# Recurrence gates of a hybrid layer as pairs of 64-row matmuls, with an explicit order of steps

## The chip, the cores and the metric

The kernel runs on one core of one Trainium2 chip. The metric is device microseconds of one execution, as a median over runs. Engines are named as in the profile: PE (TensorE matmuls), PEld (its weight loads), DVE (VectorE), ACT (ScalarE), POOL (GpSimd), SP (SyncE, which issues most DMAs). A trailing q ("SPq") is an engine's sequencer, which issues DMAs and waits.

## The reference

One layer on 512 positions of width 1024, in float32. A normalised input goes through one large projection whose columns serve three mixers (pooling, a gated linear recurrence, stick-breaking attention) and three sets of gates; the mixers' outputs are projected, gated, summed, projected and added to the input; a SwiGLU feed-forward follows. The change lies in the recurrence:

```python
def rglru_mixer(u, conv_w, conv_b, w_rg, b_rg, w_ig, b_ig, lru_lambda):
    ...
    xc = conv_b + conv_w[0] * up[:, 0:S]
    for k in range(1, CONV_WIDTH):              # 4 taps, causal, per channel
        xc = xc + conv_w[k] * up[:, k:k + S]
    xb = xc.reshape(B, S, LRU_BLOCKS, LRU_BLOCK)    # 16 blocks of 64 channels
    r = jax.nn.sigmoid(jnp.einsum('bshi,hij->bshj', xb, w_rg)... + b_rg)
    i = jax.nn.sigmoid(jnp.einsum('bshi,hij->bshj', xb, w_ig)... + b_ig)
    log_a = (-LRU_C * r) * jax.nn.softplus(-lru_lambda)
    a = jnp.exp(log_a)
    mult = jnp.sqrt(-jnp.expm1(2.0 * log_a))
    b = mult * (i * xc)
    _, h = lax.associative_scan(combine, (a, b), axis=1)   # h[t] = a[t] h[t-1] + b[t]
```

## The kernel before

Channels lie on the 128 partitions, positions along the free dimension. Every large product is made of three matmuls (`mm3`): both operands are split into a rounded part (fp32r, "h" or "hi") and a residue ("l" or "lo"), and h·h, h·l and l·h are summed in PSUM. Splitting a weight costs an ACT instruction (`whi`, L99) and a DVE instruction (`wlo`, L100). Weights come in half-chunks of 512 KB through SP's DMA queue; a list `specs` gives their order, and `weights` keeps about three of them made ahead, at a scheduling priority 200 instructions earlier (`AHEAD`).

The program is written for a scheduler: every engine's order follows from the order in which instructions are emitted, shifted by `tc.high_priority(n)` to n instructions earlier, and by what is ready and which buffers are free in the scheduler's own reckoning. [...]

The recurrence has four chunks of 256 channels, two halves j of 128 channels each. `lru_chunk(c)` emits the projection matmuls (four steps of 12 matmuls, one step per weight half and j) into one PSUM tile (`ps_lru`), then small steps follow as closures in the list `bg`; after each step of 12 matmuls `tick` takes one closure from the list, or two where it holds more than 8. The steps are: the first tap with bias (L529), three more taps (`conv`, L536), the split (`xch` L542, `xcl` L543), for each j the two gates (`gates`: three matmuls for r, three for i, into the tile `lg`; sigmoids L553), `tanh` (L557, L560), then in `lru_late` exponent and square root (L569, L572), `lru_decay` (L577, L578), `lru_input` (L582, L583), the scan (L589) and a store to DRAM on POOL's queue (L593). A gate weight holds two blocks of 64 x 64 on the diagonal of a 128 x 128 matrix whose other half is zero.

Between the four chunks stand the chunks of the second branch's gates (`gate1`), then the seven-product query, key and value projections (`tok_product`, products named 11, 12, S2, S1, S3, S4, 22), which need sums of weights on DVE (L148) and of the normalised input (`prepare_t`). PSUM holds four tiles of two banks (`pb`); SBUF tiles of 4 KB per partition come from tags w (8), t (8) and b (13).

At the start, `warm` matmuls run while the first loads come. The first product (L610) goes over eight slices k of the input: `xt` slice k, its scaled and rounded form `hu` (L362, L363), and weights `whi`, `wlo` (L380, L383, later L99, L100). The vector constants `vt` are loaded in two parts, the first weights for k = 0 in two parts.

Of the kernel before, what the change touches and what calls it, by code (L numbers as in the profile page):

```python
# [8 lines left out]
F32 = mybir.dt.float32  # L9
# [17 lines left out]
NEG = -1.0e30  # L27
WARM = 7
# [5 lines left out]
PAD = 104  # L34
# [28 lines left out]
def layer_kernel(ctx: ExitStack, tc: tile.TileContext, x, xt, vecs, w_in, w_pool, w_rg, w_ig,  # L63
# [113 lines left out]
    for n in (0, 1, 4, 2, 3, 5, 6, 7):  # L177
        if n < 4:
            add_lru(n)
        else:  # L180
            add_gate(1, n - 4)
# [151 lines left out]
    with ExitStack() as first:  # L333
# [34 lines left out]

# [3 lines left out]
        src0 = cols(w_in, 0, 2, 5120, 512)  # L372
        for k in range(2):
            load_xt(k)
            for n in ((0, 2),) if k else ((0, 1), (1, 2)):
                q = slice(256 * n[0], 256 * n[1])
                if n == (0, 1):
                    nc.scalar.dma_start(vt[:, 0:8], vecs[:, 0:8])
                (nc.scalar if n == (0, 1) else nc.sync).dma_start(raw0[:, k, q], src0[:, k, q])
                dve.tensor_copy(hi0[:, k, q], raw0[:, k, q])  # L380
            if k == 0:
                nc.sync.dma_start(vt[:, 8:], vecs[:, 8:])
            dve.tensor_tensor(lo0[:, k, :], raw0[:, k, :], hi0[:, k, :].bitcast(F32), ALU.subtract)  # L383
            make_h(k)
# [125 lines left out]
        lw = {}  # L510

        def load_lru_weights():
            for nm, src in (("r", w_rg), ("i", w_ig)):
                raw = wp.tile([P, 8, P], F32, tag="raw", name="rawl" + nm)
                nc.gpsimd.memset(raw, 0.0)
                bd = src.rearrange("(t two) i j -> two i t j", two=2)
                for two in range(2):
                    q = slice(64 * two, 64 * two + 64)
                    nc.sync.dma_start(raw[q, :, q], bd[two])
                hi, lo = w4([8, P], f"lwh{nm}", F32R), w4([8, P], f"lwl{nm}", F32R)  # L520
                act(hi, raw, AF.Copy)
                dve.tensor_tensor(lo, raw, hi.bitcast(F32), ALU.subtract)
                lw[nm] = (hi, lo)

        def lru_chunk(c):
            pair = chan_chunk(("lru", c), hn, 1, pb, True)
            u, xc = pair, b4([2, S], f"xc{c}")
            for j in range(2):
                act(xc[:, j, :], pair[:, j, :], AF.Identity, scale=vcol("conv_w", 24 + 2 * c + j),  # L529
                    bias=vcol("conv_b", 2 * c + j))  # L530
# [9 lines left out]
            def split():  # L540
                st["h"], st["l"] = b4([2, S], f"xch{c}", "b", F32R), b4([2, S], f"xcl{c}", "b", F32R)
                act(st["h"], xc, AF.Copy)  # L542
                dve.tensor_tensor(st["l"], xc, st["h"].bitcast(F32), ALU.subtract)  # L543
                st["r"], st["i"] = b4([2, S], f"lr{c}"), b4([2, S], f"li{c}")

            def gates(j):
                ps = pb.tile([P, 2, S], F32, tag="mm", name=f"lg{c}{j}")
                for n, (nm, bn) in enumerate((("r", "b_rg"), ("i", "b_ig"))):
                    hi, lo = lw[nm]
                    ct = 2 * c + j  # L550
                    mm3(ps[:, n, :], hi[:, ct, :], lo[:, ct, :], st["h"][:, j, :], st["l"][:, j, :],
                        True, True)
                    act(st[nm][:, j, :], ps[:, n, :], AF.Sigmoid, bias=vcol(bn, ct))  # L553
# [8 lines left out]
            return [conv, split] + [nothing] * (2 + c // 2) + [lambda: gates(0), lambda: gates(1), tanh]  # L562
# [12 lines left out]
        def lru_decay(c):  # L575
            e, t = lru[c]["r"], lru[c]["t"]
            dve.scalar_tensor_tensor(t, e, 1.0, t, ALU.add, ALU.mult)  # L577
            act(t, t, AF.Identity, scale=-1.0, bias=1.0)  # L578
# [18 lines left out]
        def lru_late(cs):  # L597
            out = [lambda: lru_exp(cs)]
            for f in (lru_decay, lru_input, lru_scan, lru_store):
                out += [lambda f=f, c=c: f(c) for c in cs]  # L600
            return out
# [27 lines left out]
        bg.extend(lru_chunk(0))  # L629
        bg.extend(lru_chunk(1))  # L630
        bg.extend(lru_late((0, 1)))
        gate1(0)
        bg.extend(lru_chunk(2))
        bg.extend(lru_chunk(3))
        bg.extend(lru_late((2, 3)))
        gate1(1)
        gate1(2)
        bg.extend(prepare_t())
# [50 lines left out]
        for t in range(3):  # L689
# [15 lines left out]
            for nm in ORDER:  # L705
# [17 lines left out]
                else:  # L723
                    final((1, 0), ps["22"])
# [611 lines left out]
```

## Time and profile before

| | |
|---|---|
| median of 3 runs | 939.86 us (939.56 to 939.95) |
| the profiled execution | 940.17 us, span 938.4 us |
| granted TensorE clock | 1.00 |
| HBM read, written | 107.01 MB, 16.25 MB |

The times in a trace count from the span's start. In the rows of stages, an engine's figure is its busy time in that stretch, with the number of instructions behind it; in the groups, the figures are total busy time, mean ns of one, and the engine's idle time just before them with what ended it. In the list of waits the three figures are total us, times, longest.

### The profile page before, as it was taken

The numbers are of one execution on the slowest core, as the hardware profiler recorded it, in microseconds if no ns is written. First come the engines' busy times: TensorE is split into PE (matmuls) and PEld (weight loads), VectorE is DVE, ScalarE is ACT, GpSimd is POOL, SyncE is SP. The second block draws the span as 40 slices with busy tenths as digits, with TensorE's granted clock in tenths as the row PEclk, the third lists the DMA queues.
The fourth block names the chain that finished last, engine by engine and source line by source line (L and its number), as shares of the span: only waits on it lengthen the run. The fifth ranks groups of instructions, "written<-read, shape, count | busy, mean of one in ns | idle before, by whom it ended". The sixth has DMA issues, their size and how long they took to land.

```text
span 938.4 us, 13033 instructions
## 1 busy us (share of the span) xinstructions
PE 927.4 (99%) x5089; PEld 798.2 (85%) x5089; DVE 702.6 (75%) x877; ACT 491.6 (52%) x660; POOL 43.1 (5%) x71
## 2 busy tenths in 40 slices
PE   8999999999999999999999999999999999999998
PEld 6887878888878888788888878889999999988898
DVE  6895859877696699866865545699888888787465
ACT  6557689445665465645633324454554555653232
POOL 1100000122211000000000000000000000000000
PEclk9999999999999999999999999999999999999999
DMA  9483434552714943256422334345533334523001
GB/s 327 127 286 92 133 113 158 193 190 71 244 63 139 283 120 124 65 161 182 143 91 89 104 123 155 91 131 147 148 92 93 110 111 128 168 93 109 1 28 64
DMA packets 127022, 124.12 MB, mean 132 GB/s; under 512 B 7408, under 2 KB 105968, under 8 KB 126960
## 3 DMA queue, kind: packets, MB, share of 16 engines
q1 hardware_dynamic: 122784, 108.99, 38.0%
q0 software_dynamic: 3888, 14.16, 4.6%
q8 instruction: 40, 0.66, 0.3%
q14 instruction: 22, 0.18, 0.1%
q10 hardware_dynamic: 288, 0.14, 0.0%
HBM read 107.01 MB, written 16.25 MB: 131 GB/s over the span
## 4 chain that ended last, share of the span: by engine, by line
PE 93%; DVE 4%; issue 1%; ACT 1%; DMA 0%; POOL 0%; SPq 0%; DVEq 0%; POOLq 0%; ACTq 0%
PE ps_y L1148 11%; PE ps_x L1148 8%; PE ps_q L683 7%; PE ps_br L225 4%; PE ps_br L227 4%; PE ps_br L226 4%; PE ps_gate L226 3%; PE ps_gate L227 3%; PE ps_gate L225 3%; PE ps_d L225 3%; PE ps_d L227 3%; PE ps_d L226 3%; PE ps_dy L1148 2%; PE ps_gate L610 2%; PE ps_dx L1148 2%; PE ps_pool L225 2%
## 5 line engine op out<-in xcount | busy, mean ns | idle before, releaser
L99 ACT ACTIVATE whi<-raw 128x1024 fp32r<-128x1024 f32 x93 | 98.4, 1058 | 151.4 <-PE ps_br L226 46.2
L100 DVE TENSOR_TENSOR wlo<-raw,whi 128x1024 fp32r<-128x1024 f32 x93 | 113.6, 1222 | 70.1 <-ACT whi L99 65.2
L1138 ACT ACTIVATE wh_S<-w_S 128x1024 fp32r<-128x1024 f32 x44 | 46.6, 1061 | 56.6 <-PE ps_y L1148 25.4
L1139 DVE TENSOR_TENSOR wl_S<-w_S,wh_S 128x1024 fp32r<-128x1024 f32 x44 | 53.6, 1221 | 12.8 <-ACT wh_S L1138 12.6
L1138 ACT ACTIVATE wh<-w 128x1024 fp32r<-128x1024 f32 x33 | 35.1, 1062 | 49.0 <-issue 12.9
L100 DVE TENSOR_TENSOR wlo<-qw,whi 128x1024 fp32r<-128x1024 f32 x36 | 43.9, 1221 | 20.6 <-ACT whi L99 20.5
L1139 DVE TENSOR_TENSOR wl<-w,wh 128x1024 fp32r<-128x1024 f32 x33 | 40.3, 1222 | 17.4 <-ACT wh L1138 17.4
L99 ACT ACTIVATE whi<-qw 128x1024 fp32r<-128x1024 f32 x36 | 38.0, 1056 | 25.9 <-PE ps_q L683 13.7
L225 PE MATMUL ps_gate<-HH,whi 128*128 128x512 f32 x128 | 50.0, 391 | 0.0
L227 PE MATMUL ps_gate<-HH,wlo 128*128 128x512 f32 x128 | 49.9, 389 | 0.0
L226 PE MATMUL ps_gate<-HL,whi 128*128 128x512 f32 x128 | 49.8, 389 | 0.0
L225 PE MATMUL ps_d<-ah,whi 128*128 128x512 f32 x112 | 43.6, 391 | 0.0
L226 PE MATMUL ps_d<-al,whi 128*128 128x512 f32 x112 | 43.6, 389 | 0.0
L227 PE MATMUL ps_d<-ah,wlo 128*128 128x512 f32 x112 | 43.6, 389 | 0.0
L1126 DVE TENSOR_TENSOR w_S<-w,w 128x1024 f32<-128x1024 f32 x22 | 26.9, 1223 | 3.3 <-PE ps_d L226 2.9
L227 PEld LDWEIGHTS ps_gate<-HH,wlo 128*128 128x128 f32 x128 | 24.0, 188 | 5.1
L225 PEld LDWEIGHTS ps_gate<-HH,whi 128*128 128x128 f32 x128 | 24.0, 188 | 5.0
L226 PEld LDWEIGHTS ps_gate<-HL,whi 128*128 128x128 f32 x128 | 24.0, 188 | 4.9
L1126 DVE TENSOR_TENSOR w_S<-w,w_S 128x1024 f32<-128x1024 f32 x22 | 26.9, 1223 | 0.6
L901 DVE TENSOR_TENSOR_SCAN E<-K,zero 128x511 f32<-128x511 f32 (+3 forms) x32 | 25.5, 813 | 1.1 <-ACT K L896 1.1
L225 PE MATMUL ps_out<-mth,whi 128*128 128x512 f32 x64 | 25.0, 390 | 0.9 <-DVE g L310 0.9
L225 PE MATMUL ps_br<-yph,whi 128*128 128x512 f32 x64 | 25.6, 400 | 0.0
(642 smaller groups left out, 3016.5 us busy)
## 6 DMA issues: line engine op xcount, KB each, us to landing
raw<-in_w_in_dram SPq DMA_DIRECT2D x39, 512.0 KB, 4.6
qw<-in_w_in_dram SPq DMA_DIRECT2D x24, 512.0 KB, 4.7
raw<-in_w_branch_dram SPq DMA_DIRECT2D x24, 512.0 KB, 3.5
w<-in_w_ffn_gate_dram SPq DMA_DIRECT2D x36, 256.0 KB, 3.7
w<-in_w_ffn_up_dram SPq DMA_DIRECT2D x36, 256.0 KB, 4.5
raw<-in_w_ffn_down_dram SPq DMA_DIRECT2D x14, 512.0 KB, 3.5
qd<-r POOLq DMA_DIRECT2D x12, 512.0 KB, 3.6
at<-qd SPq DMA_DIRECT2D x24, 256.0 KB, 5.3
```

The lines of the kernel that those rows point to most:

```text
L99: act(hi, raw, AF.Copy)
L100: dve.tensor_tensor(lo, raw, hi.bitcast(F32), ALU.subtract)
L225: nc.tensor.matmul(ps, lh, rh, start=start, stop=False, skip_group_check=skip)
L226: nc.tensor.matmul(ps, lh, rl, start=False, stop=False, skip_group_check=skip)
L227: nc.tensor.matmul(ps, ll, rh, start=False, stop=stop, skip_group_check=skip)
L610: nc.tensor.matmul(pss[n // 2][n % 2], w[:, k % 2, n * P:(n + 1) * P], hu[k][x_], start=k == 0 and w is wh and x_ == 0, stop=k == KT - 1 a ...
L683: nc.tensor.matmul(ps[:, a, :], b_[:, k, ts_], a_[:, kk, :], start=first and n == k == 0, stop=n == 2 and k == 3, skip_group_check=True)
L901: dve.tensor_tensor_scan(E[:, f - 1:c0 + n - 1][:, ::-1], K[:, f:c0 + n][:, ::-1], zero[:, 0:1].to_broadcast([P, c0 + n - f]), 1.0, ALU.mu ...
L1126: dve.tensor_tensor(t, raw[c, x], raw[c, y], op)
L1138: act(h, raw[c, nm], AF.Copy)
L1139: dve.tensor_tensor(l, raw[c, nm], h.bitcast(F32), ALU.subtract)
L1148: nc.tensor.matmul(o, a[:, w, k, :], b[:, k, :], start=first and n == k == 0, stop=n == 2 and k == 3, skip_group_check=True)
```

## The change

- Gates: the weights of r and i of one block share a 64-row, 128-column tile. For the block on partitions 0 to 63 its columns are r then i, for the block on 64 to 127 i then r, so that r comes out on the block's own partitions and i on the others. Each of the three products is then a pair of 64-row matmuls into the two banks of a tile. A half has two 64-partition sigmoids for r and two for i; the i sigmoid moves its result to the other partitions, and its bias is loaded swapped into `bigx`. The gate weights take two tiles instead of four, and need no zeros.
- First tap, rounding of xc, and the decay's last step for the first two chunks are on DVE instead of ACT; taps and split run at priority `EARLY`.
- The order of steps is written out around the chunks; input and scan of the last chunks move behind product S3 of the first projection. The third chunk of the recurrence comes ahead of `gate1(0)`.
- Head: `vt` is loaded whole and first on SP's queue; the first weights are loaded whole, for k = 0 on ACT's queue.

```diff
-        for k in range(2):
-            load_xt(k)
-            for n in ((0, 2),) if k else ((0, 1), (1, 2)):
-                q = slice(256 * n[0], 256 * n[1])
-                if n == (0, 1):
-                    nc.scalar.dma_start(vt[:, 0:8], vecs[:, 0:8])
-                (nc.scalar if n == (0, 1) else nc.sync).dma_start(raw0[:, k, q], src0[:, k, q])
-                dve.tensor_copy(hi0[:, k, q], raw0[:, k, q])
-            if k == 0:
-                nc.sync.dma_start(vt[:, 8:], vecs[:, 8:])
+        nc.sync.dma_start(vt, vecs)
+        for k in range(2):
+            load_xt(k)
+            (nc.sync if k else nc.scalar).dma_start(raw0[:, k, :], src0[:, k, :])
+            dve.tensor_copy(hi0[:, k, :], raw0[:, k, :])
...
+            raw = wp.tile([P, 8, P], F32, tag="raw", name="rawl")
+            for n, src in enumerate((w_rg, w_ig)):
                 bd = src.rearrange("(t two) i j -> two i t j", two=2)
                 for two in range(2):
-                    q = slice(64 * two, 64 * two + 64)
-                    nc.sync.dma_start(raw[q, :, q], bd[two])
+                    q, o = LH[two], LH[(n + two) % 2]
+                    nc.sync.dma_start(raw[q, :, o], bd[two])
...
+            for two in range(2):
+                nc.sync.dma_start(bigx[LH[1 - two], :], big[LH[two], :])
...
-            for j in range(2):
-                act(xc[:, j, :], pair[:, j, :], AF.Identity, scale=vcol("conv_w", 24 + 2 * c + j),
-                    bias=vcol("conv_b", 2 * c + j))
+            with tc.high_priority(EARLY):
+                for j in range(2):
+                    dve.tensor_scalar(xc[:, j, :], pair[:, j, :], vcol("conv_w", 24 + 2 * c + j),
+                                      vcol("conv_b", 2 * c + j), ALU.mult, ALU.add)
...
-                act(st["h"], xc, AF.Copy)
+                dve.tensor_copy(st["h"], xc)
...
             def gates(j):
+                ct = 2 * c + j
                 ps = pb.tile([P, 2, S], F32, tag="mm", name=f"lg{c}{j}")
-                for n, (nm, bn) in enumerate((("r", "b_rg"), ("i", "b_ig"))):
-                    hi, lo = lw[nm]
-                    ct = 2 * c + j
-                    mm3(ps[:, n, :], hi[:, ct, :], lo[:, ct, :], st["h"][:, j, :], st["l"][:, j, :],
-                        True, True)
-                    act(st[nm][:, j, :], ps[:, n, :], AF.Sigmoid, bias=vcol(bn, ct))
+                for n, (w, x_) in enumerate((("h", "h"), ("h", "l"), ("l", "h"))):
+                    for two in range(2):
+                        q = LH[two]
+                        nc.tensor.matmul(ps[:, two, :], lw[w][q, ct, :], st[x_][q, j, :],
+                                         start=n == 0, stop=n == 2)
+                for two in range(2):
+                    q, o = LH[two], LH[1 - two]
+                    act(st["r"][q, j, :], ps[q, two, :], AF.Sigmoid, bias=vcol("b_rg", ct)[q, :])
+                    act(st["i"][q, j, :], ps[o, two, :], AF.Sigmoid, bias=bigx[o, ct:ct + 1])
...
+        c0, s0, g0, t0 = lru_chunk(0)
+        bg.extend([c0, s0, nothing, nothing])
+        c1, s1, g1, t1 = lru_chunk(1)
+        bg.extend([c1, s1, g0, t0])
+        c2, s2, g2, t2 = lru_chunk(2)
+        bg.extend([c2, s2, g1, t1])
         gate1(0)
+        bg.extend([lambda: lru_exp((0, 1)), g2] + late_of(lru_decay, 0, 1))
+        c3, s3, g3, t3 = lru_chunk(3)
+        bg.extend([c3, s3, t2] + late_of(lru_input, 0))
         gate1(1)
+        bg.extend(late_of(lru_input, 1) + [g3, t3, lambda: lru_exp((2, 3))])
         gate1(2)
+        for f, cs in ((lru_scan, (0, 1)), (lru_store, (0, 1)), (lru_decay, (2, 3)), (lru_input, (2,))):
+            bg.extend(late_of(f, *cs))
         bg.extend(prepare_t())
         gate1(3)
```

48 lines of the change are left out of this document (26 added, 22 removed).

## The prediction

> **What bounds the kernel now.** I read the page's first part, then the busy time by stage around the changed steps, then who waited for whom on PE and DVE, and last the order of single instructions at the places that these named.
>
> ```profile
> span 938.4 us, 13033 instructions
> PE 927.4 (99%) x5089; PEld 798.2 (85%) x5089; DVE 702.6 (75%) x877; ACT 491.6 (52%) x660; POOL 43.1 (5%) x71
> core 0: us, PE busy (x) PEld busy (x) DVE busy (x) ACT busy (x) POOL busy (x), PEclk, DMA share, GB/s
> 51.00:76.00 25.00, 25.00 (x112) 20.70 (x111) 24.40 (x30) 14.61 (x17) 1.45 (x2) 1.00 0.83 273
> 76.00:100.00 24.00, 24.00 (x105) 19.09 (x104) 10.33 (x11) 20.82 (x27) 0.72 (x1) 1.00 0.28 88
> 100.00:125.00 25.00, 23.49 (x103) 18.94 (x102) 24.09 (x26) 13.95 (x16) 1.45 (x2) 1.00 0.48 147
> 125.00:146.00 21.00, 21.00 (x92) 16.93 (x91) 10.45 (x10) 20.20 (x25) 0.73 (x1) 1.00 0.50 159
> 146.00:180.00 34.00, 34.00 (x151) 28.15 (x150) 31.00 (x28) 22.95 (x25) 5.16 (x6) 1.00 0.41 133
> sum 129.00, PE 127.49 PEld 103.82 DVE 100.27 ACT 92.54 POOL 9.52; mean PE 25.50 PEld 20.76 DVE 20.05 ACT 18.51 POOL 1.90
> ```
>
> The recurrence lies between 51 and 180 us. PE is the bound there, with one gap (23.49 of 25 us in 100 to 125), at the granted clock 1.00. VectorE is uneven: 24.4, 10.3, 24.1, 10.5, 31.0 us; where it is full, ScalarE has room, and the other way about. So an instruction taken off PE is worth its spacing, not its duration, and work moved to VectorE is free only as long as VectorE's idle 129 - 100.3 = 28.7 us can be used.
>
> ```profile
> 168.16 5.44 PE ps_q L683 x24
> 640.15 2.83 PE ps_y L1148 x24
> 75.00:146.00 71.00, 13.91 (x48) 8.49 (x48) 10.89 (x16) 1.00 0.41 129
> 118.77 0.39 PE L225 MATMUL ps_gate<-HH,whi 128*128 128x512 f32 x1
> 120.66 0.50 PE L225 MATMUL lg<-xch,lwhr 128*128 128x512 f32 x1 [1.51 <-ACT xch L542]
> 76.71 0.39 PE L225 MATMUL ps_gate<-HH,whi 128*128 128x512 f32 x1
> 76.97 0.50 PE L225 MATMUL lg<-xch,lwhi 128*128 128x512 f32 x1
> 77.31 0.39 PE L226 MATMUL lg<-xcl,lwhi 128*128 128x512 f32 x1
> PEld lg L225 <- ACT lr L553: 1.5, 5, 0.4
> ```
>
> First two: pieces of the chain, start, length, count. A 512-column matmul with its own weight load takes 5.44 / 24 = 0.227 us of PE, a 256-column one 2.83 / 24 = 0.118 us. The third is the stage table for the gate tile lg alone: 48 matmuls (and 48 loads). The next two show PE's gap: 1.51 us, because the rounding xch sat behind the convolution. The last four show a smaller loss: the weight load of the i gate waits for the sigmoid of the r gate, five times, and the next matmul then starts 0.34 us later instead of 0.227, since its load was not taken ahead.
>
> **The change, part by part.**
>
> *Gates.* 48 matmuls of 128 rows (half of each weight is zeros) become 48 of 64 rows, in 24 pairs; the two of a pair use different halves of the array's rows and different PSUM banks. No row of this trace shows a 64-row matmul. One end: no overlap, 48 x 0.227 = 10.9 us as now. Other end: a pair takes one spacing, 24 x 0.227 = 5.4 us. Each still has its own load of 128 columns; the 256-column row shows that a load fits into 0.118 us, so a pair needs 2 x 0.118 = 0.236 us for its loads, 24 x 0.236 = 5.7 us in all. I take that, nearest to a row: -5.2 us.
> [...]
>
> *Changing between full and half rows.* `both` puts 12 half-row matmuls in one place, four times, so there are 8 changes, more if the scheduler mixes them with other matmuls, as it did with lg and ps_gate at 120 us. Lower end 0. Upper end: the last matmul has to run out (0.39 - 0.227 = 0.16 us) and the next load isn't taken ahead (0.34 - 0.227 = 0.11 us), 8 x 0.27 = 2.2 us. I take the running out alone, 8 x 0.16 = +1.3 us.
> [...]
>
> *The gaps of PE.* Convolution, rounding and residue are now all on VectorE, at a priority 300 instructions earlier, and four or five twelve-matmul steps (2.7 us each) lie between `split` and `both`. What has to fit in is per chunk:
>
> ```profile
> L536 DVE SCALAR_TENSOR_TENSOR xc<-ps_lru,vt,xc 128x511 f32<-128x511 f32 (+2 forms) x24 | 16.2, 740 | 0.1
> L543 DVE TENSOR_TENSOR xcl<-xc,xch 128x1024 fp32r<-128x1024 f32 x4 | 4.9, 1222 | 0.4 <-ACT xch L542 0.3
> L504 DVE TENSOR_TENSOR gt<-ps_gate,rb 128x512 f32<-128x512 f32 x2 | 1.3, 681 | 0.0
> L380 DVE CAST whi<-raw 128x512 fp32r<-128x512 f32 x1 | 0.4, 433 | 0.0
> L529 ACT ACTIVATE xc<-ps_lru,vt 128x512 f32<-128x512 f32 x8 | 5.7, 766 | 0.0
> L542 ACT ACTIVATE xch<-xc 128x1024 fp32r<-128x1024 f32 x4 | 4.2, 1058 | 3.0 <-DVE xc L536 3.0
> L578 ACT ACTIVATE lt<-lt 128x1024 f32<-128x1024 f32 x4 | 4.2, 1051 | 0.0
> L553 ACT ACTIVATE lr<-lg,vt 128x512 f32<-128x512 f32 x8 | 5.4, 689 | 1.3 <-PE lg L227 1.2
> ```
>
> 6 x 0.74 + two first taps of about 0.70 + a cast of at most 2 x 0.43 + 1.22 = 7.9 us, against 11 to 13.6 us. So the 1.51 us go, and so do the five waits of the i gate's load (0.1 us each), since all six matmuls of a tile now come before its sigmoids: -2.0 us, ends -2.0 and 0. What is late next: the two PSUM tiles that each `both` needs at once, of four. Eight half-row sigmoids must free them before the next `both`, 8 x 0.69 = 5.5 us of ScalarE, in 8 to 11 us in which it also rounds two or three weights. And more chunks are alive at once: at the last `both` I count about 14 tiles of kind b where there are 13, so a sigmoid may wait for a scan or a store. I put +0.8 us for such waits, ends 0 and 4 (half an 8 us distance).
>
> *VectorE and ScalarE.* VectorE gains 8 first taps (no row; 0.43 to 0.74, I take 0.70, near the two PSUM rows) 5.6 us, 4 casts of 0.87 = 3.5, and 2 decays of 0.87 to 1.22 = 1.7: together 10.8 us, 100.3 to 111.1 us. ScalarE loses 8 x 0.77 + 4 x 1.06 + 2 x 1.05 = 12.5 us and gains 16 more sigmoids; half-row ones have no row, between half and all of 0.69, and as the columns are the same I take all, 11.0 us. It stays at about 91 of 129 us. Covered by PE's matmuls, both cost nothing by themselves; if VectorE's cover goes, see the second rival.
>
> *Moved steps.* The last chunk's input and the last two chunks' scans and stores go behind product S3 of the first projection.
>
> ```profile
> L589 DVE TENSOR_TENSOR_SCAN li<-lt,ls 128x512 f32<-128x512 f32 x8 | 9.3, 1207 | 0.0
> L582 DVE SCALAR_TENSOR_TENSOR ls<-lr,ls 128x1024 f32<-128x1024 f32 x4 | 4.8, 1219 | 0.0
> L583 DVE TENSOR_TENSOR ls<-ls,li 128x1024 f32<-128x1024 f32 x4 | 4.9, 1213 | 0.0
> ```
>
> On VectorE that is 4 x 1.2 us of scans and 2.4 us of input, in front of weight residues of that stage; their stores are now on POOL's queue between the projection's own stores and the power for the norm, which VectorE waits for. VectorE is busy 31 of 34 us from 146 to 180 already, but these 7 us are among them: they are moved within it, not added. I leave their risk inside the +0.8 us. Two POOL memsets go and two 4 KB loads come on SP's queue, at 45 us, where no wait ends on them: 0.
>
> *Head.*
>
> ```profile
> 2.14 4.56 DMA xt<-in_xt_dram
> 6.73 0.73 ACT hu L362
> 8.73 1.16 PE L610 MATMUL ps_gate<-hu,whi 128*128 128x512 f32 x4 [0.47 <-DVE whi L380]
> 10.23 1.06 ACT L99 ACTIVATE whi<-raw 128x1024 fp32r<-128x1024 f32 x1 [0.63 <-DMA raw<-in_w_in_dram]
> 12.61 1.21 PE L610 MATMUL ps_gate<-hu,wlo 128*128 128x512 f32 x4
> PE ps_gate L610 <- DVE whi L380: 0.7, 2, 0.5
> PE ps_gate L610 <- DVE wlo L383: 0.2, 1, 0.2
> 1.68 0.42 SPq L382
> ```
>
> The chain goes through the second xt (issued at 2.14), and then PE runs into the next weights, whose rounding ended a wait for their DMA at 10.23. On SP's queue one issue fewer (0.42 us) stands ahead of that xt and of those weights, though the bytes ahead are the same; the first xt now stands behind vt, one issue later, and the first matmul needs a whole load. I take -0.4 us; ends -0.9 (all of PE's waits there) and +0.4.
>
> *Sum.* -5.2 + 1.3 - 2.0 + 0.8 - 0.4 = -5.5 us. The profiled execution took 940.17 us (span 938.4 and 1.8 around it), so 934.7; it stands 0.3 above the median 939.86 of the runs, so 934.4 us as a median. The measurement can tell about 0.2%, 1.9 us. All ends on the good side give -5.4 - 2.0 - 0.9 = -8.3, or 931.5. With the dearer changes (+0.9), 3 us of new waits instead of 0.8 and nothing from the head it is 937.9.
>
> **Rivals.**
>
> 1. *The pairs don't overlap.* For it: no row shows it, and the two matmuls of a pair stand in one queue with a load between them. Against it: loads do run beside matmuls (PEld 798 us inside PE's 927). The -5.2 us vanish: 934.4 + 5.2 = 939.6 us, no change. A worse form: the load of one half can't run beside a matmul of the other, 48 x 0.11 = 5.3 us more, 944.9 us.
>
> 2. *VectorE becomes the bound between 51 and 180 us* (slower). Place: conv of one chunk, about 8 us in one piece at high priority, in front of weight residues and of the products li x xc. With 111.1 us of work it must keep its idle time under 129 - 111.1 = 17.9 us, down from 28.7, to be no later than before; above that each us costs one. For it: its idle time was waiting for ScalarE:
>
> ```profile
> DVE wlo L100 <- ACT whi L99: 18.2, 8, 4.9
> DVE li L557 <- ACT li L553: 6.9, 2, 6.1
> ```
>
> and those weights are rounded only when PE frees a buffer. Against it: rounding leaves ScalarE, so that one hop is gone, and a backlog can be worked off after 180 us. If 24 us stay idle: 24 + 111.1 - 129 = +6.1 us, 945.6 us with the head's gain.
>
> **How the numbers follow.** Forecast case 0.66, with its own range 931.5 to 938 from the sums above; no overlap 0.15 (same); exposed loads 0.05 and VectorE 0.14 (both slower). Of the forecast case I give 0.64 to faster and 0.02 to same, for a small mishap that eats it; of the no-overlap case 0.13 to same and 0.02 to faster; a hundredth of the slow cases stays within 0.2%. Faster 0.66, same 0.16, slower 0.18. The range reaches from 931.5 to 941.5: it takes in the no-overlap case and leaves out most of the slow ones (0.15) and a little below.
>
> **What would show it.** Right: lg's 48 matmuls start in pairs a few ns to 0.12 us apart, the pairs about 0.24 us; no wait of PE on xch; around each `both` a gap of 0.1 to 0.3 us. Wrong: starts 0.227 us apart (first rival); gaps of PE on wlo, or on lr and li, between 76 and 185 us (second rival, or PSUM tiles); a first dense stretch of PE that begins later than 12.6 us (head).

## The result, and the profile after

The changed kernel takes 937.66 us (median of 12 executions, 936.79 to 939.15); the kernel before took 939.92 beside it (12, 939.13 to 940.15). The ratio is 0.9979, 95% interval 0.9971 to 0.9987: a gain of 2.3 us where 5.5 were forecast. The times of the changed kernel lie in two groups of six, 936.8 to 936.9 and 938.4 to 939.2; the profiled execution (936.89 us) is of the first, and what sets the groups apart is under "the head" below.

First the top of the page of the changed kernel and its busy time by stage (columns as in the stage rows of the prediction), to lay beside those of before:

```profile
span 934.8 us, 13035 instructions
PE 922.3 (99%) x5089; PEld 793.8 (85%) x5089; DVE 709.8 (76%) x889; ACT 485.7 (52%) x657; POOL 44.4 (5%) x69
51.00:76.00 25.00, 25.00 (x112) 20.72 (x111) 24.41 (x33) 9.19 (x10) 0.73 (x1) 1.00 0.80 278
76.00:100.00 24.00, 24.00 (x116) 18.82 (x115) 18.25 (x21) 18.13 (x23) 0.00 (x0) 1.00 0.30 88
100.00:125.00 25.00, 25.00 (x116) 20.18 (x115) 16.70 (x20) 21.38 (x27) 0.73 (x1) 1.00 0.35 106
125.00:146.00 21.00, 21.00 (x99) 16.85 (x98) 18.70 (x17) 18.61 (x25) 2.18 (x3) 1.00 0.52 176
146.00:180.00 34.00, 31.19 (x136) 25.09 (x135) 32.00 (x34) 21.07 (x23) 7.35 (x6) 1.00 0.45 140
sum 129.00, PE 126.19 PEld 101.67 DVE 110.06 ACT 88.38 POOL 10.99; mean PE 25.24 PEld 20.33 DVE 22.01 ACT 17.68 POOL 2.20
```

From 51 to 146 us PE now has no gap, and does 443 matmuls there where it did 412. The gap that was at 120 us is gone, and a new loss stands in the last row: 31.19 of 34 us, where before it was 34.00. The list of waits of PE names it:

```profile
PE ps_q L708 <- DVE wlo L101: 3.0, 3, 1.4
PE ps_q1S L708 <- DVE wlo L101: 0.8, 2, 0.5
```

The times at which PE issues the first matmul of some tiles, read from the two timelines, tell how much was ahead where:

| first matmul of | before, us | after, us | ahead, us |
|---|---|---|---|
| ps_lru (first chunk of the recurrence) | 50.87 | 49.84 | 1.03 |
| ps_q (first projection, Q) | 151.68 | 144.12 | 7.56 |
| ps_q0S (fourth product of Q) | 173.44 | 167.73 | 5.71 |
| ps_q1S (fourth product of K) | 228.51 | 223.81 | 4.70 |
| ps_q2S (fourth product of V) | 278.49 | 274.92 | 3.57 |
| end of the span | 938.4 | 934.8 | 3.6 |

So the recurrence gave 6.5 us between 51 and 152 us, a little more than the 5.9 us that the forecast's steps have there, and the projections, which the change doesn't touch but for the late steps of the recurrence, took 4.0 of the 7.6 us back.

*The gates.* PE around the first half-row tile, in the changed kernel:

```profile
79.54 0.39 PE L228 MATMUL ps_lru<-HH,wlo 128*128 128x512 f32 x1
79.85 0.50 PE L557 MATMUL lg<-xch,lwh 64*128 64x512 f32 x2
80.19 0.40 PE L557 MATMUL lg<-xcl,lwh 64*128 64x512 f32 x2
80.42 0.40 PE L557 MATMUL lg<-xch,lwl 64*128 64x512 f32 x2
...
81.12 0.40 PE L557 MATMUL lg<-xch,lwl 64*128 64x512 f32 x2
81.44 0.50 PE L226 MATMUL ps_lru<-HH,whi 128*128 128x512 f32 x1
81.78 0.40 PE L227 MATMUL ps_lru<-HL,whi 128*128 128x512 f32 x1
```

"x2" and 0.40 us: the two of a pair run as one (they start 3 ns apart), and the next pair follows after 0.232 us. Each change between whole and half rows costs 0.08 + 0.11 us: 0.31 to the first pair instead of 0.23, then 0.34 to the second: the load of the first pair starts 2 ns ahead of its matmuls, where in the run of pairs a load starts 0.23 us ahead.

*The place where the time went back.* PE, DVE and ACT around 150 us in the changed kernel; the number behind the start is the duration:

```profile
149.58 0.49 PE L708 MATMUL ps_q<-whi,HH 128*128 128x512 f32 x1
151.50 0.50 PE L708 MATMUL ps_q<-wlo,HH 128*128 128x512 f32 x1 [1.43 <-DVE wlo L101]
146.82 1.22 DVE L149 TENSOR_TENSOR qw<-qw,qw 128x1024 f32<-128x1024 f32 x1
147.96 1.22 DVE L594 SCALAR_TENSOR_TENSOR lt<-lr,lt 128x1024 f32<-128x1024 f32 x1
149.09 1.22 DVE L602 SCALAR_TENSOR_TENSOR ls<-lr,ls 128x1024 f32<-128x1024 f32 x1
150.23 1.22 DVE L101 TENSOR_TENSOR wlo<-qw,whi 128x1024 fp32r<-128x1024 f32 x1
146.59 1.28 ACT L501 ACT_TABLE_LOAD   x1
147.88 0.69 ACT L501 ACTIVATE gt<-ps_gate,vt 128x512 f32<-128x512 f32 x1
148.47 1.05 ACT L100 ACTIVATE whi<-qw 128x1024 fp32r<-128x1024 f32 x1
```

PE needs the low part at 149.8. DVE has a decay and an input step of the recurrence ahead of it, and ACT rounds the high part only after a table load and a sigmoid. The same low part and the matmul that needs it, before:

```profile
154.25 1.22 DVE L100 TENSOR_TENSOR wlo<-qw,whi 128x1024 fp32r<-128x1024 f32 x1
157.35 0.39 PE L683 MATMUL ps_q<-wlo,HH 128*128 128x512 f32 x1
```

Before, it was ready at 155.5, 1.9 us ahead of PE. In the changed kernel it is ready at 151.5, 4.0 us earlier, but PE needs it 7.6 us earlier: 7.6 - 4.0 - 1.9 = 1.7 us late. At 173 us the same thing happens behind the power on POOL:

```profile
167.48 3.69 POOL L255 TENSOR_TENSOR rsqq<-ssq,mhalf 128x8 f32<-128x8 f32 x1 [3.66 <-DVE ssq L680]
171.20 0.17 DVE L256 TENSOR_TENSOR qrs<-rsqq 128x8 f32<-128x8 f32 x1 [1.56 <-POOL rsqq L255]
171.29 1.22 DVE L609 TENSOR_TENSOR_SCAN li<-lt,ls 128x512 f32<-128x512 f32 x1
172.48 1.22 DVE L609 TENSOR_TENSOR_SCAN li<-lt,ls 128x512 f32<-128x512 f32 x1
173.67 1.22 DVE L101 TENSOR_TENSOR wlo<-qw,whi 128x1024 fp32r<-128x1024 f32 x1
```

DVE idles for the power, then does two scans, and the low part that PE waits for comes last: ready at 174.9 and needed at 173.4, where before it was ready at 178.3 and needed at 179.1. The power took 3.69 us, part of it beside DVE's work; the shortest of the eight in this execution took 1.64. That DVE is the reason is not shown: another of them took 1.66 us with DVE busy throughout.

*The head.* The first matmuls of the first product before, in the changed kernel, and in a profile of the changed kernel with its late steps issued later (below), which starts alike but got the full clock later:

```profile
4.78 1.16 PE L610 MATMUL ps_gate<-hu,whi 128*128 128x512 f32 x4 [0.22 <-DVE whi L380]
5.28 1.20 PE L627 MATMUL ps_gate<-hu,whi 128*128 128x512 f32 x4 [0.65 <-ACT hu L363]
5.36 2.07 PE L627 MATMUL ps_gate<-hu,whi 128*128 128x512 f32 x4 [0.73 <-ACT hu L363]
```

The third row needs 2.07 us for four matmuls: they are spaced 0.43 us, like the warm-up matmuls (0.43), and so on to 10.65 us; from 11 us on the spacing is 0.23. The stage rows print a clock of 1.00 there, because the clock records of these traces begin with the first grant of the full clock: at 5.07 us in the changed kernel's profile (4.38 before), at 10.81 in this one. The first product starts 0.5 us later than before but then runs without a gap, so that 1.0 us is won when the clock is full from 5 us on, and lost again, and more, when it isn't: in that profile the first recurrence product is at 52.46 us.

### The profile page after: what moved, and what is told of

The parts are those of the page before. It is cut to its first block, busy times and chain, and to the rows that moved or that the text cites. A ratio compares the mean times of both kernels' runs of the same rounds, so it can differ in the third digit from the quotient of the medians.

```text
span 934.8 us, 13035 instructions
## 1 busy us (share of the span) xinstructions
PE 922.3 (99%) x5089; PEld 793.8 (85%) x5089; DVE 709.8 (76%) x889; ACT 485.7 (52%) x657; POOL 44.4 (5%) x69
## 4 chain that ended last, share of the span: by engine, by line
PE 86%; DVE 7%; ACT 2%; issue 2%; POOL 2%; DMA 0%; SPq 0%; POOLq 0%; DVEq 0%; ACTq 0%
PE ps_y L1176 11%; PE ps_x L1176 8%; PE ps_br L226 5%; PE ps_br L228 4%; PE ps_br L227 4%; PE ps_q L708 4%; PE ps_d L226 3%; PE ps_d L228 3%; PE ps_d L227 3%; PE ps_gate L226 2%; PE ps_gate L227 2%; PE ps_gate L228 2%; PE ps_dy L1176 2%; PE ps_gate L627 2%; DVE wlo L101 2%
```

## The experiments

All were timed beside the kernel before (medians 939.67 to 939.91 us). Two theories stood against each other: that the recurrence's gain is as forecast and is given back because PE comes earlier to low parts of weights which VectorE does not deliver as much earlier; and that the pairs, or the amount of work on VectorE and ScalarE, are at fault. Each expectation says which form of them is its theory A and its theory B.

**The head alone**, on the kernel before.

```diff
+        nc.sync.dma_start(vt, vecs)
...
-            for n in ((0, 2),) if k else ((0, 1), (1, 2)):
+            (nc.sync if k else nc.scalar).dma_start(raw0[:, k, :], src0[:, k, :])
```

> The kernel before with the new head alone. In the changed kernel PE reached the first matmul of the recurrence 1.0 us earlier (49.84 against 50.87 us) and the first matmul of the projections 7.6 us earlier (144.1 against 151.7), but ended only 3.6 us earlier; 4.0 us were lost in the projections, most of them in waits for VectorE's weight residues. Theory A (debt of work): between 51 and 175 us VectorE has so much to do that whatever PE gains ahead of the projections comes back as a wait for VectorE there; then the head's 1.0 us is there at the start of the recurrence and at most 0.3 us of it at the end, 939.6 us. Theory B (order): the waits come from single pieces that stand in front of a residue in VectorE's fixed order, pieces that only the changed kernel has there; then the head keeps its 1.0 us, 938.9 us.

Measured 941.44 us (939.44 to 941.92), ratio 1.001 (1.0001 to 1.0019). Four executions lie at 939.4 to 939.6 and seven at 941.2 to 941.9: 0.4 us better than before, or 1.5 worse. The profile is one of the seven, with four matmuls in 2.08 us at the start. The four lie nearer to A's 939.6 us than to B's 938.9, but no profile shows what they had gained at 51 us, so this run doesn't decide.

**The pairs alone**, in the order and on the engines of before.

> The kernel before with the paired 64-row gates alone: old order of steps, old places of first tap, rounding and decay, old head. A pair took 0.232 us in the changed kernel, and a change between full and half rows 0.2 us; here the two halves of a chunk are separate steps, so up to 16 changes, 3.2 us: PE should gain 48 x 0.227 - 24 x 0.232 - 3.2 = 2.1 us up to the projections, more if steps meet. Theory A: at most 0.7 us of that at the end, 939.2 us or more. Theory B: nearly all of it, 937.8 us; the old wait for xch at 118 us stays in both.

Measured 947.15 us, ratio 1.0072 (1.0058 to 1.0086). PE's longest waits, and the rounding that ends the first of them:

```profile
PE lg L560 <- ACT xch L550: 3.9, 1, 3.9
PE ps_gate L225 <- ACT li L565: 3.0, 1, 3.0
124.63 1.06 ACT L550 ACTIVATE xch<-xc 128x1024 fp32r<-128x1024 f32 x1 [7.35 <-DVE xc L544]
```

Neither theory has such a time. In the old order the convolution of the third chunk ends at 124.5 us on VectorE, 5 us later than before (119.5). It stands behind decay, input and scans of the first two chunks, which begin 5.1 us later (105.84 against 100.76) because ScalarE's square roots do; ahead of those ScalarE now has 16 half-row sigmoids of 0.69 us where it had 8 whole ones. That these 5.5 us are the whole cause is argued, not shown. The granted clock falls to 0.50 during the first of the two pauses and stays there from 124.0 to 137.7 us. So in the old order the pairs gain nothing: they come with more work on ScalarE.

**The six matmuls of a half one row half after the other** instead of pair by pair.

```diff
-                for n, (w, x_) in enumerate((("h", "h"), ("h", "l"), ("l", "h"))):
-                    for two in range(2):
+                for two in range(2):
+                    for n, (w, x_) in enumerate((("h", "h"), ("h", "l"), ("l", "h"))):
```

> The changed kernel with the six 64-row matmuls of a half in another order: three for one row half, then three for the other, so that of twelve only three neighbours are on different row halves. Nothing else differs. If only neighbours overlap, a step of twelve takes 9 x 0.23 = 2.1 us instead of 1.4, 2.7 us more in four steps. Theory A: PE is later into the projections and waits less there, so at most 1 us of the 2.7 shows at the end, under 938 us. Theory B: all of it shows, 939.5 us (from the changed kernel's 936.8).

Measured 937.14 us, ratio 0.9976 (0.9965 to 0.9986): no different. PE still shows pairs:

```profile
80.10 0.50 PE L557 MATMUL lg<-xch,lwh 64*128 64x512 f32 x2
80.43 0.40 PE L557 MATMUL lg<-xcl,lwh 64*128 64x512 f32 x2
```

The two of the first row are the first and the fourth in the program, 10 ns apart; the second of the program starts 0.33 us behind the first. So the edit did not take the overlap away, and did not test what it was meant to. Whether the scheduler or PE brought the two together is not shown.

**The late steps issued later**: input of the last chunk, scans and stores of the last two behind the first product of K.

```diff
-                if (t, nm) == (0, "S3"):
+                if (t, nm) == (1, "11"):
```

> The changed kernel with input of chunk 3, scans and stores of chunks 2 and 3 moved from behind product S3 of the first projection to behind product 11 of the second, some 27 us of PE later. They are 7.3 us of VectorE, four of them (scans) at 163 to 176 us around the residue for which PE waited 1.4 us. Theory A: VectorE's debt at 175 us falls by 7 us, the waits at 149 stay, those at 173 go, and the second projection has to carry them: 1 to 1.5 us faster than the changed kernel, or nothing if they come back at 224 us. Theory B: the wait at 173 goes (1.4 us), 935.4 us, and no other comes.

Measured 937.39 us (935.56 to 937.82), ratio 0.9971 (0.9959 to 0.9982). VectorE's order from 146 to 180 us came out the same, presumably since the scheduler draws these steps forward to where it reckons VectorE idle; the waits at 150 and 173 us stayed (1.42 and 1.38), those at 224 and 227 went. Here moving the place of issue was not enough to move a step. From the first recurrence product to the end of the span this profile is the shortest of all, 883.6 us against 884.9 in the changed kernel; its late clock at the start hides that.

**The old head under the rest of the change, and two more warm-up matmuls** (9 instead of 7).

> The changed kernel with the first loads and the constants placed as in the kernel before; everything else is the change. Theory A (the head is worth about 1 us where the clock is granted as early as before, and costs about 1 us where it is granted late): the times have one peak, near 937.8 us, between the two groups that the changed kernel shows (936.8-936.9 and 938.4-939.2), and the first 20 us show the half-speed matmuls that the kernel before has, no more. Theory B (the two groups come from something later, and the head has no part in them): two groups again, each moved by one and the same amount.

> The changed kernel with 9 warm-up matmuls instead of 7, so that TensorE stays busy up to 0.9 us longer before the first product. Theory A (the pause of 1.3 us before the first product, 0.8 us before the change, makes the chip grant the full clock late in some executions): one group, near 936.8 us, median 936.5-937.0, and no half-speed matmuls after 6 us. Theory B (the late grant does not hang on the pause): two groups as in the changed kernel, median 937-939.

Measured 937.29 us (936.98 to 938.09) with the old head and 937.14 (936.98 to 937.74) with 9 warm-up matmuls. Neither has a group at 938.4 to 939.2. With the old head the first product starts at 4.81 us; with 9 warm-ups PE is busy up to it, and it starts at 5.42. So the slower group, half of the executions of the changed kernel and about 2 us behind the other, goes with the pause between warm-up and first product (0.79 us before, 1.28 after, start to start). That the full clock comes late in it is read from profiles of other kernels with this head (10.81 us with the late steps issued later, 10.37 with 128-row gates, below); in the changed kernel none of the slower group was profiled. In the median the new head costs 0.4 us (937.66 against 937.29, with intervals that overlap) where a gain of 0.4 was forecast.

**Gates of 128 rows in the new order.**

> The changed kernel with gates of 128 rows (the block-diagonal weights of the kernel before, 12 matmuls of 128 rows for each chunk) in the new order. TensorE does 24 x 0.227 = 5.4 us more in the gates and saves 8 changes x 0.2 = 1.6 us: 3.8 us more. Theory A (time that TensorE gains ahead of the projections is given back there, since VectorE's chain of low parts and sums of squares sets when their weights are ready): the projections' waits for low parts of the weights (3.0 + 0.8 us) shrink by about as much and the kernel is at most 1.5 us slower than the changed one (937-939). Theory B (those waits are fixed in size, set by the order of VectorE's steps, whatever TensorE's start): the waits stay near 3.8 us and the kernel is 3.3-4.3 us slower (about 941).

Measured 939.88 us (938.05 to 940.62), ratio 0.9998 (0.9989 to 1.0007). PE's waits for low parts shrink:

```profile
PE ps_q1S L696 <- DVE wlo L101: 0.8, 2, 0.5
PE ps_q L696 <- DVE wlo L101: 0.7, 2, 0.5
```

From the first recurrence product to the first projection product PE needs 98.25 us here and 94.28 in the changed kernel: the pairs are worth 4.0 us there. From the same start to the end of the span it is 886.4 against 884.9: 1.5 us are left. That is theory A's account. Its time (937 to 939) fits four of the eleven executions, 938.1 to 938.4; the others, at 939.8 to 940.6, had the late clock at the start if they are like the profiled one (first full clock at 10.37 us).

**First tap and rounding back on ScalarE.**

> The changed kernel with the convolution's first tap and its rounding back on ScalarE (4 + 4 chunks of work, about 9 us moved from VectorE to ScalarE before 146 us). Theory A (VectorE's backlog at 146 us, made by the 9 us of moved work, is what makes TensorE wait for low parts): TensorE's waits for them at 149 and 173 us shrink below 1.5 us in sum and the time is at or below 936 unless the gates now wait for ScalarE. Theory B (the wait at 149 and 173 comes from where decay, input and scan stand in VectorE's order, not from its total): those waits stay at 2.5-3.5 us in sum. Either way a wait of the gates for the rounded half (ScalarE) is looked for: 0-4 us, as the kernel with paired gates alone had 3.9 us of it; if it appears, the time is 938-942.

Measured 941.33 us (939.28 to 941.75), ratio 1.0012 (1.0003 to 1.002). With 9 us less on VectorE the waits between 149 and 178 us grow from 2.8 to 4.2 us, more than either theory had:

```profile
PE ps_q L708 <- DVE wlo L101: 3.4, 4, 1.7
PE ps_q0S L708 <- DVE wlo L101: 1.0, 1, 1.0
149.14 1.06 ACT L100 ACTIVATE whi<-qw 128x1024 fp32r<-128x1024 f32 x1
```

The high part at 150 comes 0.67 us later, behind more work of ScalarE, so this run puts one load in place of another. It speaks against theory A, that the moved work is what makes low parts late, but alone it doesn't settle order against amount. The feared wait of the gates did not come.

**The steps held back by an edge in the program.** In four kernels with 9 warm-up matmuls an instruction is tied behind the low part issued last before it on VectorE: decay and input of chunks 2 and 3, now issued after the third sum product (first); the first step after the power, issued 8 ticks later (second); both (third); both with 128-row gates (fourth).

```diff
+    def behind(x):        # x comes after the last low part in VectorE's order
+        tc.add_manual_dep(x.ins, state["wlo"].ins.name, ...)
...
             x = dve.scalar_tensor_tensor(s_, e, 1.0, s_, ALU.add, ALU.mult)
+            if c > 1:
+                behind(x)
```

> The changed kernel with 9 warm-up matmuls, in which decay, input and scan of chunks 2 and 3 are issued after the third sum product and each held on VectorE behind the low part of the weights that was issued last before it (six steps of 1.2 us leave VectorE's stretch from 145 to 166 us). The power's four small steps stay. Compared with the kernel with 9 warm-up matmuls alone (937.14 median). Theory A (these steps stand ahead of the low parts in VectorE's order and are what TensorE waits for at 150 us): the 1.42 us wait at 150 shrinks below 0.7, and without those steps VectorE is also earlier at 173, whose 1.38 us wait shrinks or goes; time 934.8-936.2. Theory B (the wait at 150 is ScalarE's late high part, behind exponentials, square roots and two table loads): the wait stays over 1.0 us; time 936.5-937.3.

> The changed kernel with 9 warm-up matmuls, in which GpSimd's power for the sums of squares is issued 8 ticks later and the first small VectorE step that needs it is held behind the low part of the weights issued last. Decay, input and scan stay where they are. Theory A (at 173 us VectorE idles 1.56 us for the power, with the low part that TensorE needs behind it in its order): the 1.38 us wait at 173 goes or falls below 0.4, the one at 150 stays at 1.4; time 935.3-936.4. Theory B (VectorE has so much queued there that the low part is late anyway, by the two scans of 1.2 us that now stand ahead of it): the wait stays over 0.9; time 936.6-937.3.

> Both edits together on the changed kernel with 9 warm-up matmuls. Theory A (the loss behind the gates is VectorE's order): the waits for low parts in the projections (3.0 + 0.8 us) fall to about 1 us or less and the time is 933.5-935.0, near the forecast of 934.4. Theory B (VectorE or ScalarE is full there whatever the order): at most 1 us is won (936-937), new waits in other places of the projections.

> The kernel with both edits, with gates of 128 rows (the block-diagonal weights of the kernel before) instead of the pairs. TensorE then does about 4.0 us more ahead of the projections, as the rows of the kernel with 128-row gates showed (first projection 6.36 us later, of which 2.39 us are there at the first recurrence product already). Theory A (what the pairs gain was given back in the waits, 2.7 of 4.0 us): with the waits gone, the pairs are worth their full 3.5-4.0 us, so this kernel is 3.0-4.0 us slower than the one with both edits (937-939). Theory B (the given-back time is elsewhere): 1.3-1.5 us slower, as between the kernels without the edits.

| | median, us | ratio (interval) | PE's new waits |
|---|---|---|---|
| steps | 936.43 | 0.9968 (0.9955 to 0.998) | 0.76 at 150, none at 173, 2.46 at 205, 0.64 at 263 |
| power | 936.91 | 0.9971 (0.996 to 0.9983) | 1.42 at 150, 0.60 at 173, 2.12 at 278 |
| both | 937.19 | 0.9973 (0.9963 to 0.9983) | 0.76 at 150, 1.15 and 1.83 at 205 to 209 |
| both, 128 rows | 941.71 | 1.0015 (1.0006 to 1.0024) | 1.15 and 1.82 at 209 to 212 |

Each edit removes or halves the wait that it aims at, and most of what it wins is lost at the next one; the times that theory A gave were missed by all three. With the steps held back the next one is a sum of Q (`r`, L731), which stands behind the moved scans:

```profile
PE ps_q L716 <- DVE r L731: 2.5, 1, 2.5
205.78 1.21 DVE L617 TENSOR_TENSOR_SCAN li<-lt,ls 128x512 f32<-128x512 f32 x1
206.92 1.19 DVE L731 TENSOR_TENSOR r<-r,ps_q0S 128x1024 f32<-128x1024 f32 x1
```

Between the last two kernels of the table the medians differ by 4.5 us, and from first recurrence product to the end by 4.1. That is not the pairs' worth alone: behind the same two waits the clock is 0.50 for 3.41 us in the third kernel and for 6.83 us, 0.97 of them idle, in the fourth (means of the two executions 0.997 and 0.995). If half of the busy time there is lost, as the spacing of 0.43 us for 0.23 at the start has it, that is 1.7 and 2.9 us, so 1.2 of the 4.1 us are clock and about 2.9 are the pairs'. The kernel with the steps alone has the lowest median of all that were run, 936.43 (936.23 to 936.57 in four of its five executions, 938.36 in the other), 1.2 us below the changed kernel; the intervals of the two overlap.

**The steps still later**, behind the second (12) or third (S2) product of K; the former also with exponentials and square roots of these chunks issued there, and with 128-row gates.

> As the kernel whose late steps (decay, input, scan of chunks 2 and 3) are held behind low parts of the weights, but issued one group of products later, after the second product of K, so that in VectorE's order they stand behind the last sum of Q, for which TensorE waited 2.5 us at 205 us there. 9 warm-up matmuls. Theory A (the given-back time is VectorE's order alone, and it has room after 212 us): the waits at 150 (0.76) stay and those at 173, 205 and 223 are gone or under 0.5; time 934.2-935.2, near the forecast of 934.4. Theory B (the time that TensorE gains is given back at the next step that VectorE does late, wherever the late steps stand: VectorE's or ScalarE's total in 145-296 us is the limit): a new wait of 1.5-3 us after 205 us and a time of 936-937.

> The same with the late steps issued one more product later (after the third of K). Theory A: as the one before within 0.7 us (934.2-935.5), the six steps and four scans lying beside products of K, where VectorE has idle time. Theory B: a wait of 1.5-3 us at another place, 936-937.

> The first of these with the exponentials and square roots of chunks 2 and 3 issued with the late steps too. In ScalarE's order the square roots and two table loads (2.0 + 2.6 us between 143.3 and 147.9 in the changed kernel) then leave the place ahead of the high part that is ready too late at 150. Theory A (the rest of the wait at 150, 0.76 us, is ScalarE's): it goes below 0.3 and the time is 0.4-0.8 us below that of the first of these. Theory B (VectorE's sums of weights ahead of that high part make it late): the wait stays within 0.2 us of 0.76.

> The first of these with gates of 128 rows instead of the pairs. Theory A (2.7 of the 4.0 us that the pairs take from TensorE before the projections were given back in waits that VectorE's order made): now 3.0-4.0 us slower than the first of these (937.5-939). Theory B (the time given back is not that of the waits): 1.0-1.6 us slower, as 938.1-938.4 against 936.8 without the edits.

Measured 939.12, 940.38, 939.28 and 942.39 us (ratios 0.9991, 1.0006, 0.9989, 1.0028): all above the changed kernel. The first two miss the times of both theories. The waits at 173 and 205 are gone in all, and with the square roots moved the one at 150 too, as A has it; but in the first a wait of 1.36 us stands at 244 and one of 1.87 at 263. At 244 VectorE is not full:

```profile
244.01 0.17 DVE L260 TENSOR_TENSOR krs<-rsqq 128x8 f32<-128x8 f32 x1 [1.85 <-POOL rsqq L259]
244.71 1.22 DVE L101 TENSOR_TENSOR wlo<-qw,whi 128x1024 fp32r<-128x1024 f32 x1
```

It idles 1.85 us for the power, and the low part that PE waits for is next in its order. The medians contain losses of clock as well: of the eleven executions of the first, the five with a mean granted clock of 0.999 or more took 937.8 to 938.1 us, the six with 0.998 took 939.1 to 940.0. The pairs are worth 3.3 us here, as theory A has it, in the medians (942.39 - 939.12) and 3.0 in the two profiles (from first recurrence product to the end 888.9 and 885.9), both at the full clock.

**And the power's steps held back as well**, by 4 and by 2 ticks, with ScalarE's eight scalings of K tied behind the last high part.

> The kernel whose late steps are issued after the second product of K, and in which also the steps behind GpSimd's power (VectorE's four small ones and, for K, ScalarE's eight scalings) are issued 4 ticks later and held behind the parts of the weights issued last. In that kernel without this, TensorE waited 1.36 us at 244 us while VectorE idled 1.85 us for the power with the low part next in its order, and 1.87 us at 263. Theory A (order: VectorE has idle time there, and only what stands ahead of the low parts decides): the wait at 244 goes below 0.4 and the one at 263 below 1.0; time 935.0-936.3 where that kernel has 937.8-938.1 in its faster half. Theory B (VectorE and ScalarE are full: the wait moves on): the sum of TensorE's waits for low parts and for results between 140 and 300 us stays at 4 us or more, time 937 or more.

> The same with 2 ticks. In VectorE's order one low part instead of two stands ahead of the power's steps of the second K product, and the order around 255-263 us is that of the kernel without the edit. Theory A: the wait at 244 goes below 0.7, the one at 263 stays near 1.9; time 936.3-937.3 against 937.8-938.1. Theory B: no better than the kernel without it (937.8 or more).

Measured 938.12 us (935.84 to 939.02) and 939.04 (937.59 to 939.89), ratios 0.9977 (0.9968 to 0.9986) and 0.9991 (0.9982 to 1.0). The waits at 244 and 263, which theory A wanted below 0.4 and 1.0, are gone with 4 ticks; with 2 they are 0.77 and 2.32, and the time is B's. With 4 ticks PE waits nowhere between 152 and 276 us, and then

```profile
PE ps_q L720 <- ACT r L732: 3.3, 1, 3.3
277.54 1.26 ACT L704 ACTIVATE r<-r,krs 128x128 f32<-128x128 f32 x4
278.71 1.00 ACT L732 ACTIVATE r<-ps_q 128x1024 f32<-128x1024 f32 x1
279.40:282.70 3.30, 2.94 (x7) 2.36 (x8) 0.00 (x0) 1.22 (x2) 0.43 (x1) 0.50 0.44 163
```

the copy that frees PE's next bank stands behind sixteen scalings on ScalarE, and near the end of the pause the granted clock falls to 0.50 for 3.4 us (last row). Two of the eleven executions kept a mean clock of 1.00; they took 935.84 and 935.97 us, which is A's time. The median is B's, and so is the sum of the waits from 140 to 300 us, 0.8 + 3.3 us: the wait has moved on to a place where ScalarE is busy throughout, from 271.1 to 280.6 us. From the first recurrence product to the fourth product of V the kernels need:

| | us | ahead of before |
|---|---|---|
| before | 227.62 | |
| changed | 225.08 | 2.5 |
| steps held back | 224.54 | 3.1 |
| steps behind 12 | 226.04 | 1.6 |
| steps behind 12, power by 4 ticks | 220.58 | 7.0 |

So up to 271 us the whole gain of the recurrence can be kept, with the same instructions on each engine: between 51 and 271 us VectorE was busy for 184.6 and ScalarE for 140.3 of the 220 us. It was not kept to the end in any kernel: the last wait at 276 was left.

## Why the prediction was right, and where it was wrong

**Right.** The bound, the direction and the recurrence itself. The 24 pairs are 0.232 us apart (0.236 was taken): 5.6 us instead of 10.9, -5.3 for -5.2. That is 1.95 times as fast as one after the other. The 8 changes cost about 0.19 us each, 1.5 us for 1.3, though the first pair starts 0.07 us ahead of the modelled end of the matmul before it. That the size came out right is partly luck: 0.16 us were put for the running out alone, which took 0.08, and the load that isn't taken ahead, 0.11, was left out. The gap at 120 us and its wait for xch are gone; the gaps gave 2.6 us, not 2.0 (from first recurrence product to first projection product 98.25 us with 128-row gates in the new order, 100.81 before). VectorE's and ScalarE's totals from 51 to 180 us are 110.1 and 88.4 us, forecast 111.1 and 91. From 51 to 152 us these steps had to give 5.9 us and 6.5 were measured.

**The step that failed is "new waits": +0.8 us, measured 4.0**, the end of its range but not its reason. I looked for such waits inside the recurrence, at PSUM tiles and tiles of kind b, and none came there. I wrote of the moved steps that they were moved within 146 to 180 us and not added, and that VectorE was busy 31 of 34 us there already; that is right, and the conclusion wrong. If PE reaches that stretch 7.6 us earlier, what VectorE and ScalarE deliver there has to come 7.6 us earlier too, less the time by which it was ahead. The low parts of weights that are late now were ahead by only 1.9 and 0.8 us before, and they came only 4.0 and 3.4 us earlier, since VectorE was busy from 144.5 to 169.6 us without a pause. So the question "what is late next" had its answer in the instructions of that stretch. Kernels of 128-row gates show it from the other side: 4.0 us of pairs shrink to 1.5 with those waits, and come back to 3.0 at the full clock when the steps are issued behind product 12. In the profiles the terms add up: -6.5 us for the recurrence, +4.0 for what the projections took back and -1.0 for the head make -3.5, and the span is 3.6 us shorter. In the median the gain is only 2.3 us, because half of the executions lie in the slower group.

**The second rival** had the sign that I gave for it, gaps of PE on wlo between 76 and 185 us, but not its mechanism. That rival needed VectorE's 111 us of work to hold PE up until 180 us; PE is 5.7 us ahead of before at 168 us, and VectorE idles 18.9 of the 129 us. With the same work in another order the gaps up to 276 us went, but for 0.77 us at 150. It is what stands in front of each low part, not the total of the work. The first rival, that the pairs don't overlap, is refuted by the trace.

**The head** was put at -0.4 us, ends -0.9 and +0.4. Where the clock is full it gave 1.0 us at 50 us; in the median it cost 0.4, a difference that the intervals don't make certain. The wider pause behind the warm-up was in the forecast's reach ("the first matmul needs a whole load"), its effect on the clock was not.

**What stays open.** A kernel that keeps the gain up to the end was not found in these runs, so that 934.4 us could be reached is argued from the 7.0 us at 271 us, not shown.

## What to carry to other kernels

A gain on the bound engine is a debt of its suppliers: before forecasting it, go through the next stretch of that engine and ask, for every operand, how long ahead it was ready; where it was just in time, the gain ends there. Where a static order decides, look at what stands ahead of the late operand on its engine, above all a short step that waits for a slow third engine, and hold that step behind the operand with an edge; moving its place of issue may move nothing, and the next such place must be looked for at once. When two kernels differ by a few us, compare their granted clocks first.

## What the runs showed of the hardware

Around some pauses of PE the granted clock was 0.50, for 3.4 us in two of these profiles and for 13.7 us in that of the pairs alone, and those pauses cost more than their length; around one of 2.46 us it stayed full. What decides it is not shown by these runs. The means are those of the whole profiled execution:

| kernel | pauses, us | granted clock |
|---|---|---|
| steps held back | 2.46 at 205 | mean 1.000 |
| steps behind 12 | 1.36 at 244, 1.87 at 263 | mean 0.999 |
| the same, exponentials moved | 1.87 and, for a copy of ScalarE, 1.4 | mean 0.997 |
| both edits | 1.15 and 1.83, from 205 to 209 | 0.51 from 210.1 to 213.6, 1.00 on either side |
| power by 4 ticks | 3.3 at 276 | 0.50 from 279.4 to 282.7, 1.00 behind it |
| pairs alone | 3.94 and 3.04, from 122 to 132 | 0.50 from 124.0 to 137.7 |

At the start of the kernel much the same pause had two outcomes: with PE idle for 0.65 us ahead of the first product the full clock came at 5.07 us (the changed kernel), with 0.73 us at 10.81 (the third row of "the head"). With 9 warm-up matmuls and no pause PE had 10 matmuls between 6 and 8 us, where the profile with the late grant has 6. The two groups of times agree with this as far as profiles were taken; the other executions have none.

The matmuls of the two row halves started 1 to 5 ns apart in the changed kernel, and 10 ns apart in the pair looked at in the kernel whose source has them as first and fourth. A weight load of 64 rows took as long as one of 128 (medians 183 to 186 ns against 186 to 189), and a matmul too (0.39 us in both), so here half rows paid only in pairs (0.232 us a pair, 0.227 for one of 128 rows):

```profile
L557 PEld LDWEIGHTS lg<-xch,lwh x16: 182/183/184, 79.9 to 126.7; 64*128 64x128 f32 x16
L225 PEld LDWEIGHTS lg<-xch,lwhr x8: 186/188/188, 75.1 to 135.4; 128*128 128x128 f32 x8
```
